# Moving spreading matmuls, column sums, roots and staged tiles in the plan of a hybrid encoder kernel

## The chip, the cores and the metric

One core of a Trainium2 chip runs the whole kernel. The metric is the device time of one execution in microseconds (us). Engines: TensorE (PE) multiplies, VectorE (DVE), ScalarE (ACT) and GpSimd (POOL) do the elementwise work, SyncE (SP) issues most transfers, in its own order.

## The reference

2048 tokens of 1024 channels go through two layers. Each normalises, mixes tokens (layer 0 by windowed attention, layer 1 by latent attention), multiplies the mixer's output o by a gate silu(z), projects it (w_out), adds the residual, and then adds an embedding p, projected and gated by a second product (ple_w_gate) of the newly normalised stream. The stages of this change are, in each layer, from o and z to the next layer's input:

```python
    return (o * jax.nn.silu(z)) @ w_out
...
        h = h + y
        gate = jax.nn.sigmoid(rms_norm(h, ple_norm_g[i]) @ ple_w_gate[i])
        h = h + (p[i] @ ple_w[i]) * gate
    return rms_norm(h, final_norm_g)
```

and the first product of layer 1 (`proj = u @ w_in` in `mla`), in the stage called Latents below.

## The kernel before, in words

Everything is float32. A product of precise operands is three matmuls: each operand is split in a high and a low part, and `mm3` (L285, its matmuls L290 to L292) adds high by high, high by low and low by high. The stream is held transposed, channels on partitions, in tiles of 128 channels x 512 tokens; a *group* is 512 tokens, so there are four groups (tg) of eight tiles (f).

The program is a run of stages: projections and windowed attention, `Post` for layer 0, `Latents`, gates, the dense attention (`Dense`), `Post` for layer 1. `Post` has two halves. In the **front**, 32 products (4 groups x 8 tiles f) of 24 matmuls project the gated o; to each product VectorE adds the residual tile (`x_load` L804, `add`), ScalarE squares it, GpSimd adds up the squares of a group (`gather` L833), and the result is stored (L818). For groups 1 to 3 the attention's denominators must be spread over the 64 rows of each head: one *spreading matmul* per o tile (`o_spread`, L771) makes them from a row that `spread_load` (L753) brings and `spread_cut` (L763) splits; then `o_gate` (L778, L779) multiplies and `o_cut` splits o (L216 on ScalarE, L218). In the **back**, 32 products multiply the stored stream (`h_load` L887, `h_cut` L228 and L229) by the gate's weights; `mixin` scales (L922), takes the sigmoid (L927), multiplies by the embedding tile (`p_load` L904, multiply L929 on GpSimd), adds (L931) and squares (L827), `gather` L833 adds up again, `h_store` (L936) stores. In layer 1 the last group is cut in two segments of 256 columns.

For each group's norm, `sums_at` strings eight steps: the split of the added squares (`sum_split`, L216 and L218, tile blkE), two matmuls with ones (`sum_mm`, L266), a copy, a store of the row of 512 sums to memory, its read as 128 x 4 (`root_in` L862), the root in three steps (L236, ScalarE, L244 to L249), and the store of the roots (`root_out` L876, a 128 x 4 tile to 512 places of memory). The roots come back as a row on all partitions (`row_in`, L283). For the final layer `finish` (L940) multiplies by it; the very last segment does this without memory (`turn`, L950 to L987).

The order comes from `Plan`: each step is added with a time, `Plan.run` sorts by it and the steps are written out so; TensorE, VectorE, ScalarE and GpSimd keep that order. Times are in units of which 5.19 (`UNIT`) are one product. The order of SyncE's transfers is set by the scheduler, from when it takes each to be ready; SyncE then works in that order and waits where one isn't. Places in on-chip memory come from rings (`fring`), so a load into a place waits for the last reader of what lay there.

`Latents` begins where layer 0's back ends: 128 x 672 weight rows come through a ring of two places of 4 KB per partition (`stage`), which the first two token tiles (`u_load` L1130, `u_split`) and more weights (`cut_load`) share; each load is planned 4 units ahead of its split.

## Time and profile before

| | us |
|---|---|
| median of the 3 runs | 3672.93 (3672.21 to 3678.47) |
| the profiled execution: its own time | 3679.53 |
| its span in the trace | 3677.8 |
| TensorE busy | 3551.2 |
| VectorE, ScalarE, GpSimd busy | 2404.9, 2277.0, 1973.3 |

The table's busy times are of the whole span; the dense attention, from about 1700 to 3250 us of it, keeps its order but for one step. Layer 0's `Post` runs from about 840 to 1242 us of the span, the first products of `Latents` from there to 1265, layer 1's `Post` from about 3254 to the end. In a row of a timeline the bracket says how long the engine was idle before and what released it; SPq is SyncE's queue. In a row of windows the columns are the window's length, the busy time of each engine with its instructions, the granted clock of TensorE as a share of 2.4 GHz (PEclk), the mean share of the transfer engines that is busy, and GB/s.

### The profile page before, as it was taken

To read this page: it belongs to the slowest core of one execution; us is meant where nothing else is said; L and a number is where in the kernel's file an instruction comes from. 1 tells how busy PE (TensorE), PEld (TensorE's weight loads), DVE (VectorE), ACT (ScalarE), POOL (GpSimd) and SP (SyncE) were. 2 spreads that over 40 slices of the span, in tenths; PEclk is the share of its full clock that TensorE was granted. 3 is DMA by queue.
4 is the path that set the end of the run, shared out by engine and by line. 5 is a ranking of instruction groups with operands and counts; after the bars stand their busy time and mean duration, and the time that the engine had idled before them with its cause. 6 is when DMAs were issued, how large, how long until landed. Compare 5 with 4: busy or idle time off the path is not lost. (4 is left out here: it accounts for less than half of the span.)

```text
span 3677.8 us, 52432 instructions
## 1 busy us (share of the span) xinstructions
PE 3551.2 (97%) x17118; PEld 2967.2 (81%) x17118; DVE 2404.9 (65%) x4539; ACT 2277.0 (62%) x4267; POOL 1973.3 (54%) x1564
## 2 busy tenths in 40 slices
PE   8999999999899899999999999999999999989997
PEld 6888888877787798899888888888888888867776
DVE  6111169995444444514989898989898989964445
ACT  6111279994233433422989898989898989952333
POOL 5331310033333432111989898989898989953243
PEclk9999999999999999999999999999999999999998
DMA  5332378876654676654111212121212121066533
GB/s 189 134 118 89 106 208 203 199 193 200 165 142 133 162 220 220 224 163 131 36 51 35 54 36 59 35 58 36 57 36 58 36 63 36 26 193 178 173 97 106
DMA packets 380080, 428.18 MB, mean 116 GB/s; under 512 B 46287, under 2 KB 233167, under 8 KB 379102
## 3 DMA queue, kind: packets, MB, share of 16 engines
q1 hardware_dynamic: 360798, 390.75, 38.8%
q10 hardware_dynamic: 19008, 34.09, 2.5%
q8 instruction: 134, 2.20, 0.3%
q14 instruction: 140, 1.15, 0.1%
HBM read 251.65 MB, written 156.17 MB: 111 GB/s over the span
## 5 line engine op out<-in xcount | busy, mean ns | idle before, releaser
L1648 POOL TENSOR_TENSOR blkR<-blkF,blkX 128x512 fp32r<-128x512 f32 x1024 | 1351.6, 1333 | 177.8 <-PE ps L1638 51.7
L1609 DVE TENSOR_REDUCE blkF<-ps 128x1 f32<-128x512 f32 x1024 | 700.5, 684 | 77.4 <-PE ps L1605 41.6
L1640 ACT ACTIVATE blkF<-ps 128x512 f32<-128x512 f32 x1024 | 611.4, 597 | 100.1 <-PE ps L1638 51.1
L1641 ACT CAST blkX<-blkF 128x512 fp32r<-128x512 f32 x1024 | 635.5, 621 | 32.8
L1658 DVE TENSOR_TENSOR ps<-ps,blkF 128x512 f32<-128x512 f32 x896 | 615.5, 687 | 0.7
L1669 PE MATMUL ps<-blkR 128*128 128x512 f32 x1024 | 405.4, 396 | 1.1 <-POOL blkR L1648 1.1
L1668 PE MATMUL ps<-blkX,blkR 128*128 128x512 f32 x1024 | 405.2, 396 | 0.0
L290 PE MATMUL ps<-blkR 128*128 128x512 f32 (+2 forms) x888 | 341.2, 384 | 5.6 <-ACT blkR L216 5.4
L291 PE MATMUL ps<-blkR 128*128 128x512 f32 (+2 forms) x888 | 339.2, 382 | 0.6 <-DVE blkR L218 0.6
L292 PE MATMUL ps<-blkR 128*128 128x512 f32 (+2 forms) x888 | 338.9, 382 | 0.3 <-DVE blkR L218 0.3
L833 POOL TENSOR_TENSOR blkF<-blkF 128x512 f32<-128x512 f32 (+1 forms) x112 | 145.8, 1302 | 247.0 <-ACT blkF L827 236.8
L363 DVE TENSOR_TENSOR blkF<-ps,blkF 128x512 f32<-128x512 f32 x72 | 49.5, 691 | 301.4 <-PE ps L292 296.4
L218 POOL TENSOR_TENSOR blkR<-blkF,blkR 128x1024 fp32r<-128x1024 f32 (+1 forms) x39 | 73.5, 1889 | 305.6 <-ACT blkR L216 278.2
L1669 PEld LDWEIGHTS ps<-blkR 128*128 128x128 f32 x1024 | 194.7, 190 | 47.0 <-POOL blkR L1648 2.4
L1668 PEld LDWEIGHTS ps<-blkX,blkR 128*128 128x128 f32 x1024 | 194.9, 190 | 44.2
L827 ACT ACTIVATE blkF<-blkF 128x512 f32<-128x512 f32 (+1 forms) x120 | 72.2, 602 | 221.9 <-DVE blkF L812 112.3
L290 PEld LDWEIGHTS ps<-blkR 128*128 128x128 f32 x888 | 171.0, 193 | 36.9 <-ACT blkR L216 6.2
L292 PEld LDWEIGHTS ps<-blkR 128*128 128x128 f32 x888 | 170.5, 192 | 31.6 <-DVE blkR L218 1.0
L291 PEld LDWEIGHTS ps<-blkR 128*128 128x128 f32 x888 | 170.8, 192 | 29.7 <-DVE blkR L218 0.9
L223 DVE TENSOR_TENSOR blkR<-ps,blkR 128x512 fp32r<-128x512 f32 (+2 forms) x232 | 143.5, 625 | 48.9 <-ACT blkR L222 48.7
L1636 PE MATMUL ps<-blkZ 96*128 96x512 f32 x384 | 155.0, 404 | 7.8 <-ACT blkF L1640 7.8
L290 PE MATMUL ps<-blkR,blkX 128*128 128x512 f32 (+1 forms) x384 | 149.6, 390 | 11.9 <-ACT blkX L216 9.2
(272 smaller groups left out, 9030.2 us busy)
## 6 DMA issues: line engine op xcount, KB each, us to landing
h<-blkF SPq DMA_DIRECT2D x96, 256.0 KB
blkF<-h SPq DMA_DIRECT2D x80, 256.0 KB
a_qs<-blkF ACTq DMA_DIRECT2D x64, 256.0 KB
ple<-blkF SPq DMA_DIRECT2D x64, 256.0 KB
blkF<-h SPq DMA_DIRECT2D x32, 512.0 KB
b_v<-blkX SPq DMA_DIRECT2D x32, 512.0 KB
b_q<-blkX SPq DMA_DIRECT2D x64, 256.0 KB
blkZ<-b_q SPq DMA_DIRECT2D x64, 256.0 KB
```

Of the source, the lines that this page charges most:

```text
L290: mm(out, lhsT=lh, rhs=rh, start=(first and i == 0), stop=False)
L291: mm(out, lhsT=lh, rhs=rl, start=False, stop=False)
L292: mm(out, lhsT=ll, rhs=rh, start=False, stop=(last and i == n - 1))
L833: getattr(self.k.nc, eng).tensor_tensor(out=acc, in0=acc, in1=sq, op=ALU.add)
L1609: nc.vector.tensor_reduce(out=mm[:, qt, kc : kc + 1], in_=ps, axis=AX.X, op=ALU.max)
L1636: nc.tensor.matmul(sp, lhsT=kl[:, kt_], rhs=qh[0:96, :], start=True, stop=False)
L1640: nc.scalar.activation(pe, sp, AF.Exp, scale=SCALE_B)
L1641: nc.scalar.copy(ph, pe)
L1648: nc.gpsimd.tensor_tensor(out=pl, in0=pe, in1=fv(ph), op=ALU.subtract)
L1658: nc.vector.tensor_tensor(out=st["acc"], in0=prev, in1=st[kt][0], op=ALU.add)
L1668: nc.tensor.matmul(st["o"], lhsT=v, rhs=ph, start=(kt == 0), stop=False)
L1669: nc.tensor.matmul(st["o"], lhsT=v, rhs=pl, start=False, stop=(kt == NT - 1))
```

## The change

- `o_spread` of group 1 is put in pairs before products 3 to 6 of group 0; of a later group each before the product of the same number in the group before. Its loads, the spread row's load and split, and `o_cut` move with it.
- Roots and their stores are put 6 units later behind each column sum (`SUMS`); the front's column sums of groups 0 to 2 come 3 units later (`PS_SS`), the back's 3.5 (`PS_SB`), the back's gathers 2.15 (`GATHB`), `finish` 6 more, `x_load` 2.23 earlier, `h_load` of groups 1 to 3 two earlier.
- The ring of residual tiles (`xrs`) gets a fourth place, that of the second root row.
- `Latents`: weights in three places of 2.625 KB, the first token tile in two halves and the second in one piece with places of their own, and a table of load and split times (`L_AT0`).
- In `Dense` the last unit's reciprocal is put 4 units later.

```diff
@@ -33,19 +33,23 @@
...
 UNIT = 5.19
-PS_X, PS_EV, PS_ST, PS_SS, PS_H, PS_P, PS_HS, PS_SB = 2.17, 0.61, 2.06, 6.29, 1.2, 3, 0.68, 6.5
-L_FIRST, L_PACE, L_CUT = -32, 2.6, (9.44, 10.74, 22.24, 26.4, 32.24)
+PS_X, PS_EV, PS_ST, PS_SS, PS_H, PS_P, PS_HS, PS_SB = 4.4, 0.61, 2.06, 9.3, 1.2, 3, 0.68, 10
+L_AT = {c: 2.625 * (c % 3) for c in range(8)} | {("u", 0): (28, 36), ("u", 1): 0} | {("cut", "r", c): 5.25 for c in range(3)}
+L_AT |= {("cut", "v", 0): 0, ("cut", "v", 1): 4, ("cut", "q", 0): 0, ("cut", "q", 1): 4, ("cut", "q", 2): 0}
+L_AT0 = [(-36.2 + 2.65 * c, -30 + 2.65 * c) for c in range(8)] + [(-30, -9.5), (-11, 2.5)]
+L_AT0 += [(-10, -5), (-4.5, 0.5), (0.7, 6), (3, 9.44), (6.2, 10.74), (16, 22.24), (19, 26.4), (26, 32.24)]
+L_U2 = -14
 L_US, PS_SL = -0.33, 6.5
...
 PREP, PLE_LD = 3, 12
-PS_O1 = 15.5
 PS_WL, PS_OL, PS_OL2, PS_HL, PS_R1, PS_R2 = 4, 4, 3.72, 3.96, 2.57, 3
-L_LD, L_UL, L_KR, L_VS, L_QS, L_NS = 4, 4, 3, 1.8, 1.8, 1.8
+L_UL, L_KR, L_VS, L_QS, L_NS = 4, 3, 1.8, 1.8, 1.8
 G_WL, G_UL, G_R, G_ST = 4.5, 4.5, 3.5, 2.2
...
 D_LAT, D_RR, D_W = 19, 20, 21
-SUMS = (3, 4.2, 5, 7.5, 10.5, 10.7, 13, 14)
+SUMS = (3, 4.2, 5, 7.5, 16.5, 16.7, 19, 20)
+CUTAT, GATHB = (2.7, 1.9), 7.05
 G_W, G_U = (-15.79, -9, 2, 8), -9.81
...
@@ -693,7 +697,7 @@
...
         self.selspot = ("R", 92) if self.final else ("Y", 12)
-        self.xrs, self.sqs, self.faccs, self.baccs = k.fring(18, 20, 22), k.fring(26), k.fring(24, 14), k.fring(*baccs)
+        self.xrs, self.sqs, self.faccs, self.baccs = k.fring(18, 20, 22, rows[1]), k.fring(26), k.fring(24, 14), k.fring(*baccs)
         self.lasts = k.fring(4, 6)
...
@@ -864,16 +868,16 @@
...
-            self.st["r"] = self.k.root_end(self.st["root"], out)
+            self.st["r", i, g] = self.k.root_end(self.st["root", i, g], out)
...
@@ -1021,22 +1025,23 @@
...
                 if tg > 0:
-                    to = NC8 * (tg - 1) * UNIT + (PS_O1 + 3.2 * f if tg == 1 else 4.7 * f + 4)
-                    add(to - PS_OL2 - (4.2 if tg > 1 else 3.3), self.o_load, tg, f)
-                    add(to - 0.6, self.o_spread, tg, f)
+                    before = 3 + f // 2 if tg == 1 else NC8 * (tg - 1) + f
+                    to = (3 + f / 2 if tg == 1 else before) * UNIT + 0.6
+                    add(to - PS_OL2 - (6 if tg > 1 else 1.3), self.o_load, tg, f)
+                    add(before * UNIT - 0.01, self.o_spread, tg, f)
                     add(to, self.o_gate, tg, f, "both")
-                    add(to + 1.9, self.o_cut, tg, f, "both")
+                    add(to + CUTAT[tg > 1], self.o_cut, tg, f, "both")
                     if f == 0:
-                        add(to - 7, self.spread_load, tg)
-                        add(to - 2, self.spread_cut, tg)
-            self.sums_at(add, NC8 * (tg + 1) * UNIT + PS_SS, 1, tg)
+                        add(to - 9, self.spread_load, tg)
+                        add(to - 4.5, self.spread_cut, tg)
+            self.sums_at(add, NC8 * (tg + 1) * UNIT + (PS_SS if tg < NG - 1 else 6.29), 1, tg)
         t = NG * NC8 * UNIT
...
                 th = tb - NC8 * UNIT + (0.5 + 0.8 * f if tg == 0 else 1.2 + 0.75 * f) * UNIT + PS_H
-                add(th - PS_HL, self.h_load, tg, f)
+                add(th - PS_HL - (0 if tg == 0 else 2), self.h_load, tg, f)
                 add(th, self.h_cut, tg, f)
...
@@ -1047,7 +1052,11 @@
...
                     add(te + dt, self.mixin, g, f, i)
-                add(te + (4.9 if n == TG else 3), self.gather, 2, g, f, "vector" if last else "gpsimd")
+                if last or g == len(self.segs) - 1 and f == NC8 - 1:
+                    dt = 4.9 if n == TG else 3
+                else:
+                    dt = GATHB if n == TG else 3.7
+                add(te + dt, self.gather, 2, g, f, "vector" if last else "gpsimd")
                 t += unit
...
@@ -1068,7 +1077,7 @@
...
             if self.final and n == TG:
-                fin = t + PS_SB + 20
+                fin = t + PS_SB + 26
                 add(fin - 3, self.row_in, 2, g)
...
@@ -1098,7 +1107,7 @@
...
         self.k = k
-        self.stage, self.xts, self.cfs = k.fring(0, 4), k.fring(8, 21), k.fring(29, 32)
+        self.xts, self.cfs = k.fring(8, 21), k.fring(29, 32)
         self.uhs, self.uls = k.ring(("R", 36), ("R", 44)), k.ring(("R", 40), ("R", 48))
...
@@ -1111,8 +1120,7 @@
...
     def load(self, key, src):
-        wf = self.stage.tile([P, D])
-        wf = wf[:, : src.shape[-1]]
+        wf = self.k.at(("F", L_AT[key]), [P, src.shape[-1]])
         self.k.nc.sync.dma_start(wf, src)
...
@@ -1126,13 +1134,22 @@
...
         k = self.k
-        xt = (self.stage if t < 2 else self.xts).tile([P, NC8, P])
-        k.nc.sync.dma_start(xt, k.h1[:, t * P : (t + 1) * P].rearrange("(c p) t -> p c t", p=P))
-        self.st["u", t] = xt
+        src = k.h1[:, t * P : (t + 1) * P].rearrange("(c p) t -> p c t", p=P)
+        if t == 0:
+            xs = [k.at(("F", kb), [P, 4, P]) for kb in L_AT["u", 0]]
+        else:
+            xs = [k.at(("F", L_AT["u", 1]), [P, NC8, P]) if t == 1 else self.xts.tile([P, NC8, P])]
+        n = NC8 // len(xs)
+        for i, x in enumerate(xs):
+            k.nc.sync.dma_start(x, src[:, n * i : n * i + n])
+        self.st["u", t] = xs
     def u_split(self, t):
-        self.us[t] = self.uhs.tile([P, NC8, P], F32R), self.uls.tile([P, NC8, P], F32R)
-        self.k.split_sbuf(self.st.pop(("u", t)), *self.us[t])
+        u = self.us[t] = self.uhs.tile([P, NC8, P], F32R), self.uls.tile([P, NC8, P], F32R)
+        xs = self.st.pop(("u", t))
+        n = NC8 // len(xs)
+        for i, x in enumerate(xs):
+            self.k.split_sbuf(x, *[v[:, n * i : n * i + n] for v in u])
...
@@ -1321,12 +1338,10 @@
...
-        first = [(self.w_load, self.w_split, c) for c in range(NC8)] + [(self.u_load, self.u_split, 0)]
         cuts = [(self.cut_load, self.cut, w, c) for w, n in (("r", 3), ("v", 2), ("q", 3)) for c in range(n)]
-        first += cuts[:3] + [(self.u_load, self.u_split, 1)]
-        times = [L_FIRST + L_PACE * i for i in range(len(first))] + list(L_CUT)
-        for t, (load, cut, *args) in zip(times, first + cuts[3:]):
-            add(t - L_LD, load, *args)
+        first = [(self.w_load, self.w_split, c) for c in range(NC8)] + [(self.u_load, self.u_split, i) for i in range(2)] + cuts
+        for (t0, t), (load, cut, *args) in zip(L_AT0, first):
+            add(t0, load, *args)
             add(t, cut, *args)
...
@@ -1338,7 +1353,7 @@
...
                 if t + 2 < NT:
-                    add(e - L_UL, self.u_load, t + 2)
+                    add(L_U2 if t == 0 else e - L_UL, self.u_load, t + 2)
                     add(e + (L_US if t == 0 else 0.5), self.u_split, t + 2)
...
@@ -1751,8 +1766,9 @@
...
             plan.add(t0 + NT + DENAT + DLAG, self.spread, u)
-            plan.add(t0 + NT + RECIPAT, self.recip, u)
-            plan.add(t0 + NT + RECIPAT + ILAG, self.store_recip, u)
+            tr = t0 + NT + RECIPAT + (4 if u == nu - 1 else 0)
+            plan.add(tr, self.recip, u)
+            plan.add(tr + ILAG, self.store_recip, u)
             if h % 2 == 1 and h + 1 < HEADS and g < 2:
```

Three places show how the rows move. (In the changed kernel's file the same lines have numbers higher by 4, from L1130 on by more: L876 is L880, L1116 is L1124, L1130 is L1144.)

SyncE in the middle of layer 0's front, around the store of group 0's roots (`rs`) and the read of its row; L737 and L734 load z and o tiles for the spread groups, L804 residuals, L818 stores, L717 a weight. Before:

```order
L737 DMA blkF<-a_z 128x512
L876 DMA rs_94<-blkF 128x4x1
L734 DMA blkF<-a_o 128x512
L818 DMA h_85<-blkF 128x512
L283 DMA blkF<-rs_94 128x512
L804 DMA blkF<-in_c_xT 128x512
L737 DMA blkF<-a_z 128x512
```

and after:

```order
L741 DMA blkF<-a_z 128x512
L822 DMA h_85<-blkF 128x512
L880 DMA rs_94<-blkF 128x4x1
L738 DMA blkF<-a_o 128x512
L808 DMA blkF<-in_c_xT 128x512
L287 DMA blkF<-rs_94 128x512
L741 DMA blkF<-a_z 128x512
L822 DMA h_85<-blkF 128x512
L738 DMA blkF<-a_o 128x512
```

Before, the z and o tile right ahead of and behind the store are number 6 of group 2; after, all of group 2's tiles are ahead and the o tile between store and read is group 3's first.

GpSimd at the start of layer 0's back: L779 is the last gate of the front, L833 (L837) the gathers, L929 (L933) the multiplies by the embedding. Before:

```order
L779 TENSOR_TENSOR blkF<-blkF 128x512
L833 TENSOR_TENSOR blkF<-blkF 128x512 x9
L929 TENSOR_TENSOR blkF<-blkF 128x512 x2
L833 TENSOR_TENSOR blkF<-blkF 128x512
L929 TENSOR_TENSOR blkF<-blkF 128x512
```

and after:

```order
L783 TENSOR_TENSOR blkF<-blkF 128x512
L837 TENSOR_TENSOR blkF<-blkF 128x512 x9
L933 TENSOR_TENSOR blkF<-blkF 128x512 x3
L837 TENSOR_TENSOR blkF<-blkF 128x512
L933 TENSOR_TENSOR blkF<-blkF 128x512
```

A product's gather stood right behind its own multiply's chain and ahead of the next multiply; now it stands behind the next product's.

SyncE at the end of layer 0's back; L1116 (L1124) are the weights of Latents, L1130 (L1144) its token tiles, L904 (L908) embedding tiles, L936 (L940) stores, L876 (L880) a store of roots. Before:

```order
L1116 DMA blkF<-in_b_w_in 128x672
L1130 DMA blkF<-h_87 128x8x128
L904 DMA blkF<-ple_83 128x512
L1116 DMA blkF<-in_b_w_in 128x672
L936 DMA h_87<-blkF 128x512
L876 DMA rs_95<-rcol 128x4x1
L1116 DMA blkF<-in_b_w_in 128x672
L1145 DMA blkF<-in_c_rope 128x512
L904 DMA blkF<-ple_83 128x512
L1116 DMA blkF<-in_b_w_in 128x672
L936 DMA h_87<-blkF 128x512
L1130 DMA blkF<-h_87 128x8x128
```

and after, the first token tile's two halves:

```order
L1124 DMA blkF<-in_b_w_in 128x672
L1144 DMA blkF<-h_87 128x4x128
L908 DMA blkF<-ple_83 128x512
L940 DMA h_87<-blkF 128x512
L1124 DMA blkF<-in_b_w_in 128x672
L908 DMA blkF<-ple_83 128x512
L940 DMA h_87<-blkF 128x512
L1144 DMA blkF<-h_87 128x4x128
L1124 DMA blkF<-in_b_w_in 128x672
```

and further on the second token tile:

```order
L1162 DMA blkF<-in_c_rope 128x512
L880 DMA rs_95<-rcol 128x4x1
L908 DMA blkF<-ple_83 128x512
L940 DMA h_87<-blkF 128x512
L1144 DMA blkF<-h_87 128x8x128
```

The first token tile's load stood behind five weights, and now its halves stand behind the second and third; the second's stood 6 rows behind the store of roots and now stands 3 behind it, with the third tile's load ahead of both (not shown).

## Rows read from the trace of the kernel before

**Rows 1.** The page, busy time of each engine (its share of the span)

```profile
PE 3551.2 (97%) x17118; PEld 2967.2 (81%) x17118; DVE 2404.9 (65%) x4539; ACT 2277.0 (62%) x4267; POOL 1973.3 (54%) x1564
```

**Rows 2.** TensorE's timeline, three places: start, length, line, operation, [idle before <-releaser]

```profile
876.13 0.39 PE L290 MATMUL ps<-blkR 128*128 128x512 f32 x1
...
881.80 0.39 PE L290 MATMUL ps<-blkR 128*128 128x512 f32 x1
...
897.59 0.65 PE L771 MATMUL ps<-blkY 128*128 128x512 f32 x1 [2.56 <-DVE blkY L763]
898.03 0.63 PE L290 MATMUL ps<-blkZ,blkR 128*128 128x512 f32 x1
...
3663.91 0.28 PE L291 MATMUL ps<-blkR,blkY 128*128 128x256 f32 x1
3664.03 0.28 PE L292 MATMUL ps<-blkR,blkY 128*128 128x256 f32 x1
```

**Rows 3.** Windows of the six stages, as the table's text explains

```profile
887.46:1047.19 159.73, 144.43 (x600) 116.24 (x598) 73.01 (x98) 46.04 (x72) 52.33 (x39) 0.95 0.71 173
1091.22:1241.76 150.54, 140.60 (x584) 113.95 (x583) 62.85 (x96) 58.89 (x89) 58.06 (x45) 0.94 0.54 146
1241.76:1265.30 23.54, 15.12 (x76) 13.90 (x75) 10.35 (x12) 11.19 (x20) 16.24 (x13) 0.85 0.60 184
3304.69:3454.12 149.43, 140.47 (x599) 114.01 (x598) 73.53 (x98) 46.03 (x72) 52.25 (x39) 0.98 0.66 177
3498.15:3598.45 100.30, 92.75 (x389) 74.72 (x388) 48.08 (x72) 35.85 (x56) 37.76 (x30) 0.97 0.34 97
3598.45:3677.80 79.35, 55.54 (x395) 53.31 (x393) 42.49 (x101) 26.92 (x55) 27.04 (x31) 0.84 0.36 110
```

**Rows 4.** Waits of TensorE, layer 0's front: us in total, times, longest

```profile
PE ps L771 <- DVE blkY L763: 5.0, 2, 2.6
...
PE ps L266 <- DVE blkE L218: 3.2, 1, 3.2
```

**Rows 5.** SyncE's timeline in layer 0's front

```profile
924.38 0.38 SPq L876 DMA_DIRECT2D rs<-blkF  x1
...
934.70 0.32 SPq L283 DMA_DIRECT2D blkF<-rs  x1
```

**Rows 6.** GpSimd's timeline at the same place

```profile
936.49 1.28 POOL L779 TENSOR_TENSOR blkF<-blkF 128x512 f32<-128x512 f32 x1 [4.63 <-DMA blkF<-a_o]
```

**Rows 7.** Waits of TensorE, layer 0's back

```profile
PE ps L266 <- ACT blkE L216: 9.7, 3, 4.5
```

**Rows 8.** Timeline of all engines at the first column sum of layer 0's back

```profile
1099.81 0.68 DVE L922 TENSOR_TENSOR blkF<-ps,blkF 128x512 f32<-128x512 f32 x1
...
1103.86 0.69 DVE L922 TENSOR_TENSOR blkF<-ps,blkF 128x512 f32<-128x512 f32 x1
...
1104.75 1.26 POOL L833 TENSOR_TENSOR blkF<-blkF 128x512 f32<-128x512 f32 x1 [1.53 <-ACT blkF L827]
...
1106.04 0.62 ACT L216 CAST blkE<-blkF 128x512 fp32r<-128x512 f32 x1 [1.44 <-POOL blkF L833]
```

**Rows 9.** Waits of TensorE, the start of Latents

```profile
PE ps L290 <- ACT blkR L216: 4.0, 1, 4.0
```

**Rows 10.** ScalarE's timeline there, the split of the second token tile

```profile
1254.03 1.04 ACT L216 CAST blkR<-blkF 128x1024 fp32r<-128x1024 f32 x1 [1.78 <-DMA blkF<-h]
```

**Rows 11.** Waits of TensorE, the last 16 products and the end

```profile
PE ps L970 <- DVE blkF L249: 9.5, 2, 7.4
```

**Rows 12.** The chain that ended last: start, length, step

```profile
3629.08 9.97 DMA rs<-blkF
...
3639.07 5.42 DMA blkF<-rs
...
3667.07 0.44 DVE blkF L833
```

**Rows 13.** VectorE's timeline at the same place

```profile
3644.51 0.75 DVE L940 SCALAR_TENSOR_TENSOR blkZ<-blkZ,gam,blkF 128x512 f32<-128x512 f32 x1 [0.26 <-DMA blkF<-rs]
```

14 lines of the change are left out of this document (7 added, 7 removed).

## The prediction

> **What bounds the kernel now.** I read the head of the page first: TensorE is busy for 97% of the span [rows 1] of 3677.8 us, which is 1.7 us less than the profiled execution's own time of 3679.53 us. So TensorE is the bound, and what a change of order can give is the time in which TensorE stands still or runs slowly. Next I took its full pace from its timeline: a product of 24 matmuls of 512 columns and the one spreading matmul behind it take 5.67 us (881.80 - 876.13) [rows 2]. That is 0.2267 us an instruction, 5.44 us a product. Behind a wait of 2.56 us the pace is half: 0.44 us from 897.59 to 898.03 [rows 2]. The windows show such slow stretches as granted clocks of 0.84 to 0.98 in the mean [rows 3], a mix of the two levels of 2.4 and 1.2 GHz.
>
> The stages that the change touches have a window each. Instructions times 0.2267 us, taken from the window's length, is what was lost there: layer 0's front groups 1 to 3, 159.73 - 600 x 0.2267 = 23.7 us; its back groups 1 to 3, 150.54 - 584 x 0.2267 = 18.1; layer 1's front, 149.43 - 599 x 0.2267 = 13.6; its back groups 1 and 2, 100.30 - 389 x 0.2267 = 12.1. The first three products of Latents are 72 matmuls of 336 columns (0.149 us each by that pace) and 4 others: 23.54 - 11.6 = 11.9. The last 16 products are half as wide, 0.12 us a matmul (3664.03 - 3663.91) [rows 2]: they take 3664.15 - 3598.45 = 65.7 us where 384 x 0.12 and 1.1 for seven others would do, 18.5 lost; behind the last of them come 13.65 us to the end of the span. Sum: **98 us** that can be had. It is more than the waits alone, since the slow pace behind them counts too.
>
> What ends the waits? In layer 0's front it is mainly these. L771, the spreading matmul, waits twice, 5.0 us in all, for the last operation of its row's split (L763), and L266, the column sum, 3.2 us for its accumulator's [rows 4]. Other products (L290) wait for o tiles that were cut late, and behind that stands SyncE's queue: the root's write L876 is issued at 924.38, the row's read L283 can't go until 934.70 because it reads what was written, and SyncE takes its work in order, so every load behind stands still for 10 us [rows 5]. The o tile whose load was issued between the two keeps GpSimd waiting 4.63 us, to 936.49 [rows 6]. So a write of 2 KB, in 512 elements of four bytes, costs some 10 us of queue and slows the transfers beside it.
>
> The Trainium skill, DMA: Bandwidth & Descriptors, section Anatomy of one DMA, fits one transfer by about 2.0 us and its bytes over 436 GB/s; by it this write would be over in 2 us, and moving it would bring nothing. The rows measured 10.3 us from issue to the read behind it, so here the trace decides.
>
> **The change, part by part.**
>
> *Front products (both layers).* The same matmuls are issued; none is added or taken away. Group 1's spreading matmuls now stand in pairs before products 3 to 6 of group 0, the others singly before the product of the same number, and their row's load and split 2 to 2.5 units earlier (a unit of the plan is about 1.05 us, since 5.19 units are one product of 5.44). The row's split came 2.5 us late twice [rows 4]; 2.5 units take all of that. Roots go 6 units later, so the root's write stands behind the loads of group 2's last tiles, not ahead of them. The order shows it: after, one o, one x load stand between write and read, and all of group 2's z and o tiles are ahead. The 10 us of queue stay, but the loads behind are then those of group 3's tiles, used a group (43.5 us) on. The column sum goes one product later: 5.44 us against 3.2 us waited; TensorE's next product covers it. x loads go 2.23 units earlier with a fourth place in their ring; that place is the second row's, so this row's read moves behind the last x store, at the start of back group 0 and a group (43.5 us) ahead of its first use. I cost it at nothing: back group 0 hides it, and without that cover it is the 5.42 us of a row's read [rows 12]. Bounds: 0 (every wait moves on) to 23.7 + 13.6. Each wait that I named gets more room than it lasted, which lies near the upper end; an eighth I leave for slow starts: **21 + 12**.
>
> *Back products.* Column sums wait 9.7 us in 3, the longest 4.5 [rows 7]. Why: group 0's last product ends at 1091.22 [rows 3], its gather L833 starts at 1104.75, 13.5 us later, where the plan has 5.5 units; the accumulator's split begins when it ends, 1106.04. VectorE is catching up, since its evacuations L922 start 4.05 us apart and products end 5.44 apart [rows 8]. The change does two opposite things: the sum goes 3.5 units later, which the order turns into one whole product, 5.44 us; but the gather goes 2.15 units later too, behind the next product's multiply L929. While the engines lag, that multiply's operand is there, and it costs its 1.3 us: net 5.44 - 1.3 = 4.1 us, against waits of 3.2 in the mean and 4.5 at most. Without the lag it would come a product later and net 1.4 units, but then the sum waits for nothing. A square's place in its ring of three is asked back 3.35 units after the gather, so nothing waits for that. Bounds 0 to 18.1; near the upper one, less the slow starts that are left, I take three quarters, **14**. In layer 1, where the h loads come 2 units earlier, late h splits are part of the 12.1; **8** of it.
>
> *Latents.* ScalarE's split of the second token tile waits 1.78 us for its load, and TensorE 4.0 us for the split [rows 9, 10]. After, the first two tiles have places of their own and are loaded 20.5 and 13.5 units ahead of their splits, not 4; the order shows the first one's halves ahead of most weights. The second's load still stands behind a root's write, and its split is 3.3 units later. Weights use three places of 2.6 KB, not two of 4, so a load waits for the split three before it, not two. Bounds 0 to 11.9; I take 70%, **8**.
>
> *End of layer 1.* The chain goes through the root's write (9.97 us) and the read of the row (5.42 us) [rows 12]; from 3644.51 VectorE has eight finishing steps L940 of 0.75 us [rows 13] in the midst of the next group's root, and L970 waits for that, 7.4 us at the longest [rows 11]. After, the row is read behind the ple load before the last four, and lands by my estimate some 48.5 us after the start of the last 16 products (now 46.1: 3644.51 - 3598.45), near the last product. VectorE's steps from there (8 x 0.75 = 6 us, and as much of the last products' own) take 12 us, and from the last gather to the end it is 10.7 us as now (3677.80 - 3667.07) [rows 12]. 48.5 + 12 + 10.7 = 71.2 us against 79.35 [rows 3]: **8**, a half of the 18.5 that TensorE alone could save, since here VectorE, not TensorE, would end last. Bounds: all of 18.5, or 6 lost if the steps stand wholly behind the present end.
>
> *Dense.* The last unit's reciprocal goes 4 units later. Group 3 of layer 1 needs it first, 16 products (87 us) on, and these hide it: 0.
>
> Sum: 21 + 12 + 14 + 8 + 8 + 8 = 71. From this I take 11 for waits that the order lets me expect in place of the old: rows (2,0) and (2,1) still come to VectorE with 8 steps (6 us) ahead of a column sum (2 each), the second token tile (2), and the slow pace after such half-cured stalls (5, 0.21 us an instruction more for 24). **Forecast: 60 us less.** The profiled execution is 6.6 us over the median of the runs shown, 3672.93; against the median, 3613.
>
> **The rivals.**
> - *The front alone (18%).* Back sums and the end don't gain: the lag moves with the sum, since the gather was moved with it. For: both were moved, by 2.15 and 3.5 units. Against: in TensorE's order the sum moved by a whole product. Then 21 + 12 + 8 and less 3 for new waits = 38: 3673 - 38 = 3635.
> - *New waits take most (8%).* The earlier loads meet the weights' in the front (DMA share 0.71 there [rows 3]) and o tiles land late; the front gains half of its 33, the rest is lost to the same in the back: 15, 3658.
> - *Nothing moves (5%).* The root's block lies elsewhere in the queue and stalls something else there. Against: each wait gets more room than it lasted. Within 7.3 us of 3673. By the Trainium skill's fit (above) it would be so too, since a write of 2 us holds nothing up; the trace's 10.3 us speak against it.
> - *Slower (5%).* Eleven root writes have a row's read behind them (four front groups in either layer, three back groups of layer 1). If what is queued behind each is needed at once, 10.3 us each is 113 us, against the 98 now lost: 15 more, 3688. It decides from 98/11 = 8.9 us uncovered at each. For: the later place is nearer to the read in the back groups, where the next h and p loads are behind it. Against: those loads have 2 units more, and before, where the write was as long, all the stalls together came to 98.
>
> **The numbers.** The forecast's own case has 64%. Its range, by the bounds above, is a gain of 45 to 83: 3590 to 3628. With the front alone, and half of the smaller gains, the range goes to 3648 (a gain of 25). A measurement of this kernel tells 0.2%, 7.3 us, from no change. Faster: 64 + 18 + 8 = 90%; same 5%; slower 5%.
>
> **What would show it.** Right: the same windows come out at 139 and 138 us (front), 137 (layer 0's back), 15 (Latents), the granted clock of the fronts goes to 0.98 or more, the rows L771 and L266 leave the list of waits or fall under 1 us; SyncE's row read still stands 10 us behind its write, with nobody waiting; the end's L970 waits under 2 us. Wrong: L266 keeps 2 to 4 us a time in the back groups (the lag moved along), L290 waits for o or h splits behind SyncE's block, or the last product is followed by over 16 us of finishing. If the fronts gain under 20 together, my reading of the root's write as their cause is wrong.

## The result and the profile after

The changed kernel takes 3625.4 us (median of 4 runs, 3623.12 to 3625.78) where the kernel before takes 3675.7 on the same chip (4 runs, the profiled one among them): 0.9861 of it, 95% interval 0.9849 to 0.9873, or 50 us less. Measured once more on another chip it was 0.9878 (0.9862 to 0.9895), 44 us less. Forecast were 60 us less, with a range from 25 to 83.

The same six windows as in [rows 3], of the changed kernel, in the same order; the columns are the same.

```profile
884.95:1020.47 135.52, 135.52 (x598) 112.08 (x597) 70.13 (x94) 43.71 (x68) 49.71 (x37) 1.00 0.69 201
1064.50:1198.93 134.43, 133.15 (x583) 109.09 (x582) 79.39 (x93) 57.81 (x89) 61.11 (x45) 1.00 0.60 162
1198.93:1221.69 22.76, 14.23 (x76) 13.44 (x74) 12.38 (x15) 11.04 (x20) 14.64 (x15) 0.78 0.59 167
3262.67:3398.15 135.48, 135.48 (x598) 112.09 (x597) 68.84 (x93) 43.33 (x67) 48.77 (x37) 1.00 0.65 189
3442.18:3538.73 96.55, 91.03 (x389) 74.50 (x388) 60.65 (x69) 36.06 (x56) 43.10 (x30) 0.96 0.31 91
3538.73:3623.70 84.97, 52.76 (x395) 50.17 (x393) 47.82 (x102) 25.16 (x52) 27.40 (x29) 0.81 0.36 112
```

Both fronts run from end to end at 100% of the clock with TensorE busy for the whole window: 24.2 and 13.95 us less. Layer 0's back gives 16.1. The start of Latents gives 0.8, layer 1's back 3.75, and the last stage is 5.6 us **longer**. Together that is 53.2 of the 54.1 us between the two spans (3677.8 and 3623.7); of the rest, 2.5 us were gained ahead of the first window and 1.6 lost between the two layers. So the gain came where it was forecast in both fronts and in layer 0's back; at Latents it did not come, and in layer 1's back and end together 1.9 us were lost.

What waits are left? TensorE's waits of the changed kernel, first from 1190 to 1240 us, the start of Latents, then from 3420 us to the end:

```profile
PE ps L294 <- ACT blkR L220: 6.7, 1, 6.7
```

```profile
PE ps L954 <- DVE blkF L837: 13.5, 1, 13.5
PE ps L270 <- ACT blkE L220: 11.7, 2, 6.2
```

L771 and L266 (now L775 and L270) are gone from the fronts' lists, as was to be seen. But L270 stands 11.7 us in the second back, where the kernel before's same wait (L266) came to 6.2, and the last column sum (L954) stands 13.5 us behind the last product. VectorE's timeline shows where it stands, at the first finishing step L944 of each row:

```profile
3490.10 0.75 DVE L944 SCALAR_TENSOR_TENSOR blkF<-blkF,gam 128x512 f32<-128x512 f32 x1 [3.77 <-DMA blkF<-rs]
...
3544.84 0.75 DVE L944 SCALAR_TENSOR_TENSOR blkZ<-blkZ,gam,blkF 128x512 f32<-128x512 f32 x1 [5.94 <-DMA blkF<-rs]
...
3599.50 0.75 DVE L944 SCALAR_TENSOR_TENSOR blkZ<-blkZ,gam,blkF 128x512 f32<-128x512 f32 x1 [7.03 <-DMA blkF<-rs]
```

Each time VectorE stands 3.8 to 7.0 us until the row has come from memory, with the evacuations of the back products behind it in its queue. In the kernel before it stood there too, longer for the first two rows and not for the third, which is the one that [rows 13] shows (0.26 us):

```profile
3540.06 0.75 DVE L940 SCALAR_TENSOR_TENSOR blkF<-blkF,gam 128x512 f32<-128x512 f32 x1 [9.64 <-DMA blkF<-rs]
...
3592.37 0.75 DVE L940 SCALAR_TENSOR_TENSOR blkZ<-blkZ,gam,blkF 128x512 f32<-128x512 f32 x1 [8.99 <-DMA blkF<-rs]
```

In all it is 18.9 us before and 16.7 after. What is new is the third wait, and that the finishing steps stand nearer to the next column sum: they were put 9.5 units later, the sum 3.5.

### The profile page after: what moved, and what is told of

Its sections match the earlier page's. It is cut to its first block, busy times and chain, and to the rows that moved or that the text cites. A ratio compares the mean times of both kernels' runs of the same rounds, so it can differ in the third digit from the quotient of the medians.

```text
span 3623.7 us, 52443 instructions
## 1 busy us (share of the span) xinstructions
PE 3522.8 (97%) x17118; PEld 2949.7 (81%) x17118; DVE 2453.7 (68%) x4539; ACT 2277.4 (63%) x4268; POOL 1987.7 (55%) x1565
## 4 chain that ended last, share of the span: by engine, by line
PE 84%; DVE 6%; DMA 3%; ACT 2%; issue 2%; POOL 1%; SPq 0%; ACTq 0%; DVEq 0%; POOLq 0%
PE ps L296 13%; PE ps L294 13%; PE ps L295 13%; PE ps L1620 7%; PE ps L1653 6%; PE ps L1651 6%; PE ps L1683 6%; PE ps L1652 6%; PE ps L1684 6%; PE ps L601 2%; PE ps L615 1%; DVE blkF L935 1%; PE ps L557 1%; PE ps L556 1%; PE ps L616 1%
## 5 line engine op out<-in xcount | busy, mean ns | idle before, releaser
L222 POOL TENSOR_TENSOR blkR<-blkF,blkR 128x512 fp32r<-128x512 f32 (+1 forms) x40 | 74.0, 1855 | 302.2 <-ACT blkR L220 274.9
L1684 PEld LDWEIGHTS ps<-blkR 128*128 128x128 f32 x1024 | 195.0, 190 | 46.9 <-POOL blkR L1663 2.3
L837 POOL TENSOR_TENSOR blkF<-blkF 128x512 f32<-128x512 f32 (+1 forms) x112 | 159.5, 1424 | 99.3 <-ACT blkF L831 98.3
L933 POOL TENSOR_TENSOR blkF<-blkF 128x512 f32<-128x512 f32 (+1 forms) x70 | 85.8, 1225 | 223.2 <-ACT blkF L931 192.5
L294 PEld LDWEIGHTS ps<-blkR 128*128 128x128 f32 x888 | 168.0, 189 | 34.5 <-ACT blkR L220 3.1
L296 PEld LDWEIGHTS ps<-blkR 128*128 128x128 f32 x888 | 167.6, 189 | 31.6 <-DVE blkR L222 1.2
L295 PEld LDWEIGHTS ps<-blkR 128*128 128x128 f32 x888 | 167.9, 189 | 28.2
```

The lines of the kernel that those rows point to most:

```text
L294: mm(out, lhsT=lh, rhs=rh, start=(first and i == 0), stop=False)
L295: mm(out, lhsT=lh, rhs=rl, start=False, stop=False)
L296: mm(out, lhsT=ll, rhs=rh, start=False, stop=(last and i == n - 1))
L1684: nc.tensor.matmul(st["o"], lhsT=v, rhs=pl, start=False, stop=(kt == NT - 1))
```

## The experiments

Twelve kernels ran; each ratio is to the kernel before, run beside it. Windows of a stage are compared with a second trace of the changed kernel, from the run `changed_again`, since they repeat to 2 us where whole runs on different chips differ by more.

**The changed kernel again.**

> The changed kernel itself once more, for a comparison on the same chip as the other runs of this call. All theories: a ratio to the kernel before of 0.986 within 0.003, and stage windows within 1.5 us of the first trace's (front groups 1 to 3 135.5 and 135.5, back of layer 0 134.4, start of Latents 22.8, last stage 85).

Measured: 3620.74 us, 0.9878 (0.9862 to 0.9895). Its windows of layer 0's back, the start of Latents, layer 1's back and the last stage:

```profile
1062.95:1195.61 132.66, 132.43 (x584) 109.18 (x582) 78.56 (x91) 56.69 (x87) 61.05 (x46) 1.00 0.58 158
1195.61:1217.68 22.07, 14.73 (x75) 13.95 (x74) 12.86 (x17) 11.56 (x21) 13.39 (x14) 0.77 0.57 176
...
3438.26:3533.11 94.85, 90.02 (x389) 73.78 (x388) 59.31 (x69) 36.09 (x56) 41.03 (x29) 0.98 0.32 92
3533.11:3618.60 85.49, 53.20 (x395) 50.81 (x393) 48.88 (x102) 25.17 (x52) 27.68 (x30) 0.83 0.36 111
```

The windows are the same within 1.8 us, a little over the 1.5 expected.

**The spreading matmuls put back.**

```diff
-before = 3 + f // 2 if tg == 1 else NC8 * (tg - 1) + f
-to = (3 + f / 2 if tg == 1 else before) * UNIT + 0.6
+to = NC8 * (tg - 1) * UNIT + (15.5 + 3.2 * f if tg == 1 else 4.7 * f + 4)
...
-add(before * UNIT - 0.01, self.o_spread, tg, f)
+add(to - 0.6, self.o_spread, tg, f)
...
-add(to - 4.5, self.spread_cut, tg)
+add(to - 2, self.spread_cut, tg)
```

> The changed kernel with the spreading matmuls, their loads, gates and cuts put back where they stood before; all else as changed. Theory S (the places of the spreading matmuls and the earlier split of their row cured the front): the waits of the spreading matmul for its row's split, some 5 us in two, come back in either layer, with their slow starts; the windows of front groups 1 to 3 go from 135.5 us each to 143 to 150, the time goes up by 12 to 25 us. Theory R (the root's write in SyncE's queue was the cause): the windows stay within 3 us of 135.5, the time within 6 us of the changed kernel's.

Measured: 3649.03 us, 0.9959 (0.9944 to 0.9974), 30 us of 44 given back. The fronts' windows, and TensorE's waits there in layer 0 and in layer 1 (before the change: [rows 3, 4]):

```profile
885.13:1032.29 147.16, 139.24 (x600) 113.04 (x598) 67.31 (x96) 44.67 (x70) 52.02 (x38) 0.99 0.68 186
...
3275.85:3417.79 141.94, 138.20 (x599) 113.08 (x598) 68.15 (x96) 44.91 (x70) 52.94 (x38) 0.99 0.65 185
```

```profile
PE ps L775 <- DVE blkY L767: 4.4, 2, 2.6
```

```profile
PE ps L775 <- DVE blkR L767: 2.6, 1, 2.6
```

Theory S holds in the main: the first wait, 2.6 us as before, is back in both layers, and the fronts cost 11.7 and 6.5 us more. In layer 1 it is one wait, not two, and the window stays a microsecond under the 143 expected. This is a half of what the fronts gained (24.2 and 13.95). The run puts the loads, gates and cuts of the o tiles back too, so the other half, which it leaves cured, does not hang on their places alone. The time rose by more than the 12 to 25 us expected: of the 25.5 us between this trace's span and the changed kernel's the fronts are 18 and the back products some 7.

**The fronts' roots put back.**

```diff
-for dt, (f, *args) in zip(SUMS, steps):
+for dt, (f, *args) in zip((3, 4.2, 5, 7.5, 10.5, 10.7, 13, 14) if i == 1 else SUMS, steps):
```

> The changed kernel with the fronts' roots, their stores and the reading of the row put back (6 units earlier); the back's stay. Theory R (the root's write, 10 us of SyncE's queue ahead of needed o tiles, was the cause of the second half of the front's stalls): the front window of layer 0 goes from 135.5 to 144 to 148, layer 1's to 139 to 142, the time up by 12 to 17 us. Theory S (the spreading matmuls' places are what counts; the earlier loads of o tiles cover a 10 us block anyway): both windows within 2 us of 135.5, the time within 4 us.

Measured: 3648.61 us, 0.9961 (0.9949 to 0.9973). The price came, but in another place. Layer 0's front and back, and layer 1's back:

```profile
886.29:1023.33 137.04, 136.13 (x599) 111.90 (x597) 61.28 (x83) 40.45 (x63) 44.34 (x35) 1.00 0.65 188
1074.08:1215.37 141.29, 135.91 (x584) 110.65 (x582) 82.38 (x96) 59.98 (x92) 64.67 (x48) 0.98 0.56 160
...
3458.94:3561.10 102.16, 92.12 (x390) 74.88 (x388) 64.34 (x74) 38.52 (x60) 45.66 (x32) 0.95 0.31 88
```

The fronts lose 1.5 us and nothing. What loses is the back: layer 0's groups 1 to 3 8.6 us and layer 1's 7.3, and the first groups, which lie ahead of those windows, 6.7 (50.75 in place of 44.03, by the products' starts) and 3.0 (47.04 in place of 44.02). That is 25 of the 28 us between this run and the changed kernel's. So Theory S holds for the fronts' windows, and its "time within 4 us" falls. Theory R is not decided by it, since the edit hardly moved the root's write: the first is issued 34.8 us after the window's start (921.04) where the changed kernel's stands 36.0 behind it (919.44 - 883.44), the second within 0.3 us of its place, and the third comes 10 us later. VectorE shows why. Its idle time before a root's first step (L240), until the sums have been read from memory, in all and in how many times, of the changed kernel and then of this one; and the third of these waits in layer 0:

```profile
  DMA blkF<-sq: 20.9, 6
```

```profile
  DMA blkF<-sq: 66.6, 8
```

```profile
1019.96 0.17 DVE L240 TENSOR_SCALAR blkF<-blkF 128x4 f32<-128x4 f32 x1 [11.85 <-DMA blkF<-sq]
```

The step asks for the sums before they have come, VectorE keeps its order, and the evacuations behind it wait: 11.85 us at one time, at the root of group 2. In the kernel before these waits came to 20.3 us in 9, though the roots stood as near to their sums as here. VectorE was late there: to the first of these steps it came 29.0 us after the window's start (916.41), and here after 21.6 us (917.12 less the 9.22 that it waited), with the sums there at 30.8. So over the whole trace the later roots did not shorten these waits; they kept them from growing now that VectorE is less late.

**One front root a layer put back, that of the last group.** The edit is the same with `i == 1 and g == NG - 1`.

> The changed kernel with one front root a layer put back 6 units earlier: that of the last group, whose read of the sums falls in the last front products. Theory V (what putting the fronts' roots back cost, 22 us in the back windows, comes from VectorE standing at that one root's first step until the sums' row is read from memory, 11.9 us there, just when the back's first splits are due): VectorE's wait there is 8 to 12 us again, layer 0's first back group 48 to 51 us in place of 44.0, its back groups 1 to 3 138 to 142 in place of 132.7, the time up by 12 to 22 us. Rival A (all four roots are needed for it): every window within 2 us of the changed kernel's.

Measured: 3628.35 us, 0.9885 (0.9868 to 0.9902), which alone is not distinguishable from the changed kernel. VectorE's wait at that step was 1.09 us in layer 0 and 2.99 in layer 1 (none in the changed kernel), not 8 to 12. Layer 0's first back group stayed at 44.02, groups 1 to 3 and layer 1's back cost 3.3 and 4.3 us:

```profile
1066.07:1202.03 135.96, 133.63 (x584) 109.00 (x583) 80.97 (x94) 57.91 (x89) 62.81 (x47) 1.00 0.59 160
...
3446.49:3545.64 99.15, 91.02 (x390) 73.99 (x389) 62.90 (x72) 37.27 (x58) 44.88 (x32) 0.97 0.32 91
```

```profile
1041.21 0.17 DVE L240 TENSOR_SCALAR blkF<-blkF 128x4 f32<-128x4 f32 x1 [1.09 <-DMA blkF<-sq]
```

My theory named the wrong root. The wait of 11.85 us (1019.96) falls ahead of the end of the front products (1023.33), so it is the root of group 2, which this run left in its later place. The last group's root makes 7.6 of the 25 us in the backs; the rest lies with the three roots ahead of it or with all four together, and no run put group 2's back alone.

**Layer 0's back roots put back.** The same with `i == 2 and not self.final`.

> The changed kernel with the back roots of layer 0 alone put back 6 units earlier. Theory V (the back's column sums were late because VectorE stood 2.0 to 2.7 us at each root's first step, waiting for the sums' read, as in the kernel before; with the roots later it doesn't): these waits come back, and with them waits of 1 to 4 us before a group's column sum, back groups 1 to 3 at 137 to 144 us in place of 132.7, the time up by 4 to 11 us. Rival B (in the back the roots' place is of no account; the gain came from the last front root and from the earlier loads of the stream): windows within 2 us, the time within 4 us.

Measured: 3635.17 us, 0.9909 (0.9892 to 0.9926), 0.3% over the changed kernel. The back of layer 0, and the longest of the three waits of VectorE at the root's first step that came back (the others are 1.41 and 1.57 us):

```profile
1065.64:1207.51 141.87, 135.53 (x584) 109.94 (x582) 74.77 (x91) 55.73 (x86) 56.39 (x43) 0.99 0.59 143
```

```profile
1192.02 0.17 DVE L240 TENSOR_SCALAR blkF<-blkF 128x4 f32<-128x4 f32 x1 [4.13 <-DMA blkF<-sq]
```

This window is 9.2 us longer, and the start of Latents 3.1 (25.19). The two intervals touch by a hair, so the windows decide, which repeat to 2 us. Theory V holds: in layer 0's back, where VectorE no longer waits for the sums at all, that is what the later roots are worth.

**The column sums put back, with the gathers.** Two runs: the gathers alone, and the sums with them, the roots' times kept.

```diff
-CUTAT, GATHB = (2.7, 1.9), 7.05
+CUTAT, GATHB = (2.7, 1.9), 4.9
...
-dt = GATHB if n == TG else 3.7
+dt = GATHB if n == TG else 3
```

> The changed kernel with the back's gathers put back 2.15 units earlier, ahead of the next product's multiply on GpSimd; the column sums stay a product later. Theory L (the sum's later place alone covers the lag; the gather's place costs or gives a microsecond): back windows within 2 us, the time within 4 us of the changed kernel's. Rival G (GpSimd, waiting for the square with the next multiply behind it, lengthens each product's chain, so the lag was cured by the gather's move): the back windows of layer 0 go from 134.4 to over 140, the time up by 8 to 15 us.

```diff
-PS_X, PS_EV, PS_ST, PS_SS, PS_H, PS_P, PS_HS, PS_SB = 4.4, 0.61, 2.06, 9.3, 1.2, 3, 0.68, 10
+PS_X, PS_EV, PS_ST, PS_SS, PS_H, PS_P, PS_HS, PS_SB = 4.4, 0.61, 2.06, 9.3, 1.2, 3, 0.68, 6.5
...
-for dt, (f, *args) in zip(SUMS, steps):
+for dt, (f, *args) in zip((3, 4.2, 5, 7.5, 20, 20.2, 22.5, 23.5) if i == 2 else SUMS, steps):
...
-fin = t + PS_SB + 26
+fin = t + PS_SB + 29.5
```

> The kernel with the gathers put back, and the back's column sums put back 3.5 units too; the steps of the roots behind them stay at the times they have in the changed kernel. So against the kernel with the gathers back alone only the sums and their way through memory move. Theory L (the back's gain came from TensorE reaching the sum a product later): the sums' waits come back, 2.5 to 4.5 us each in layer 0, that window goes from 132.1 to 142 to 150, layer 1's back groups 1 and 2 from 92.6 to 97 to 101, the time up by 12 to 22 us. Rival V (it came from VectorE, which no longer waits for the sums' read at the root's first step): both windows within 3 us, the time within 5 us.

Measured: 3612.27 us (0.9861, 0.9845 to 0.9878) and 3613.34 (0.9859, 0.9844 to 0.9873). The second ran beside the changed kernel and is 7.4 us faster; of the first, on another chip, the ratio says 6 us and the spans of the traces 7.5. The windows of layer 0's back, the start of Latents, layer 1's back and the last stage are 0.6, 2.2, 2.3 and 5.8 us less than the changed kernel's. Three of them, of the first:

```profile
1065.03:1197.11 132.08, 132.08 (x584) 109.27 (x582) 60.48 (x92) 56.74 (x87) 60.03 (x46) 1.00 0.60 160
...
3438.85:3531.41 92.56, 90.10 (x389) 73.89 (x388) 46.84 (x68) 36.12 (x56) 38.87 (x29) 0.98 0.33 94
3531.41:3611.10 79.69, 51.72 (x395) 49.38 (x393) 42.15 (x101) 24.65 (x51) 25.27 (x29) 0.85 0.37 119
```

and layer 0's back of the second:

```profile
1065.94:1198.69 132.75, 132.52 (x584) 109.20 (x582) 60.02 (x92) 57.39 (x89) 59.93 (x46) 1.00 0.59 160
```

Two expectations fell. That the sum comes a product later is worth nothing beside the later roots: with it put back the window is 132.75, within 0.7 us, so Theory L is refuted and V holds. And the gather's later place, thought to cost or give a microsecond, costs 6 to 7 us; by the windows more than half of it lies in the last stage. The mechanism stands in two rows. The changed kernel's GpSimd and VectorE at one product (timeline of all engines):

```profile
1067.30 1.29 POOL L837 TENSOR_TENSOR blkF<-blkF 128x512 f32<-128x512 f32 x1
1067.38 1.76 DVE L935 TENSOR_TENSOR blkF<-blkF 128x512 f32<-128x512 f32 x1 [2.07 <-POOL blkF L933]
```

GpSimd goes from the multiply straight into the gather, VectorE's add starts 0.08 us later and takes 1.76 us. With the gather put back the add stands alone and takes 0.69 us (1065.34). Over the 40 adds of this shape and place the groups of instructions say the same, of the changed kernel and of the one with the gathers back (busy time, mean ns):

```profile
L935 DVE TENSOR_TENSOR blkF<-blkF 128x512 f32<-128x512 f32 x40 | 58.8, 1469 | 42.9 <-POOL blkF L933 42.9
```

```profile
L935 DVE TENSOR_TENSOR blkF<-blkF 128x512 f32<-128x512 f32 x40 | 27.5, 688 | 53.2 <-POOL blkF L933 53.1
```

The gather's 1.29 and the add's own 0.69 one after the other make 1.98; less the 0.08 that had gone by, 1.90, so the 1.76 is nearly all of it: the two hardly overlap. The Trainium skill, SBUF — State Buffer, section SBUF: two separate sides, has it as a rule: VectorE and GpSimd share a port pair, held by one instruction to its end, and a VectorE operation with two inputs in SBUF needs it. The trace agrees here, with 0.69 us alone and 1.76 beside the gather. It does not agree wholly where the add begins 0.5 us behind the gather, as at 9 of the 24 gathers of the run `changed_again` from 1038 to 1189 us:

```profile
1071.87 1.74 POOL L837 TENSOR_TENSOR blkF<-blkF 128x512 f32<-128x512 f32 x1
```

```profile
1072.38 1.77 DVE L935 TENSOR_TENSOR blkF<-blkF 128x512 f32<-128x512 f32 x1
```

There GpSimd, which began first, takes 1.74 us in place of 1.29, and the two end 2.28 us after the start of the first, not 1.98.

**Layer 1's back roots put back, the finishing steps left late.** The edit of the roots with `i == 2 and self.final`.

> The changed kernel with the back roots of layer 1 alone put back 6 units earlier, while the finishing steps stay at their later place, so that a row has 12 units from its root's store to its first use, not 6. Theory W (VectorE waits for the row at the first finishing step, 3.8, 5.9 and 7.0 us, and what stands behind it makes the column sums and the end late): these waits shrink to under 3 us each, the column sums' waits of 5.5 and 6.2 us to under 3, the last stage from 85 us to 76 to 80, the time down by 10 to 16 us. Rival N (the eight finishing steps themselves, 6 us and more of VectorE, make it late, whenever the row comes): the sums wait as long, the time within 4 us of the changed kernel's.

Measured: 3616.65 us, 0.9871 (0.9857 to 0.9886), which alone is not distinguishable from the changed kernel. The expected 10 to 16 us did not come: the ratios say 3, the spans 2.7, and layer 1's back groups 1 and 2 stayed at 94.75. The trace is clear where the edit acts: VectorE's first finishing steps wait 1.01 and 1.55 us, the third not at all; the sums' waits shrink from 11.8 to 5.8 us; the last stage takes 78.33 us in place of 85.49. Against this 3.2 us more stand ahead of layer 0's windows and 1.4 between the layers, which the edit does not touch.

```profile
PE ps L270 <- ACT blkE L220: 5.8, 2, 3.5
```

```profile
3537.57:3615.90 78.33, 53.74 (x395) 51.22 (x393) 48.62 (x102) 25.27 (x52) 27.40 (x30) 0.84 0.37 120
```

Theory W holds for the waits and the last stage, with the sums' waits a little over what it said, perhaps since the gathers still lengthened VectorE's adds there; its time does not hold.

**Gathers, layer 1's column sums and roots put back together.** The edits of the gathers and of these roots, and:

```diff
-self.sums_at(add, t + (PS_SB if n * (g + 1) < T else PS_SL), 2, g)
+self.sums_at(add, t + ((6.5 if self.final else PS_SB) if n * (g + 1) < T else PS_SL), 2, g)
```

> The changed kernel with the gathers put back (worth 6 to 7 us alone) and, in layer 1's back, the column sums and roots put back to the times before, the finishing steps staying late, so that 15.5 units lie between a root's store and the row's first use. Theory W (a row that comes after VectorE asks for it is what stalls layer 1's back and end): no wait over 1 us for the first two rows, the column sums' waits under 2 us, back groups 1 and 2 at 88 to 92 us, the last stage 8 to 13 us shorter than the changed kernel's 85; the time 14 to 20 us under the changed kernel's of the last call, 3601 to 3607 if the kernel before runs at 3665. Rival N (VectorE's own work sets the pace): the time within 4 us of the kernel with the gathers put back, 3612.

Measured: 3601.92 us (3600.62 to 3604.95), 0.9818 (0.9803 to 0.9832). This is faster than both kernels: 66 us under the kernel before on that chip. Layer 1's back and the last stage, and TensorE's waits in them:

```profile
3438.01:3526.07 88.06, 88.06 (x390) 72.82 (x388) 50.13 (x71) 36.57 (x57) 38.81 (x29) 1.00 0.38 107
3526.07:3600.60 74.53, 52.56 (x395) 50.42 (x393) 42.74 (x99) 24.27 (x51) 25.43 (x29) 0.87 0.38 116
```

```profile
PE ps L974 <- DVE blkF L253: 7.8, 2, 5.7
PE ps L954 <- DVE blkF L837: 5.2, 1, 5.2
PE ps L270 <- ACT blkE L220: 1.0, 1, 1.0
```

Layer 1's back now runs without loss too (88.06 us busy of 88.06), and no finishing step is shown waiting for its row. The one wait of 5.7 us before L974 goes back to an embedding tile (`ple`): its load was issued at 3552.64, 1.2 us behind a root's write (3551.40), and GpSimd stood 7.5 us for it, to 3564.40.

**The last full group's eight finishing steps on ScalarE and GpSimd.** The edit comes on top of those of the run before.

```diff
+if g == 2:
+    self.gain(g, f)
+    self.k.nc.gpsimd.tensor_tensor(out=hf, in0=hf, in1=self.st["row", 2, g], op=ALU.mult)
+    return
```

> As the run before, and the eight finishing steps of the last full group are done by ScalarE (the gain) and GpSimd (times the row) in place of VectorE. Theory E (behind the last product VectorE's queue is the bound: the eight steps of 0.75 us stand between the last segment's own): from the last product's start to the end 4 to 7 us less than in the run before. Rival P (GpSimd takes over as the bound, 1.3 us a step between the multiplies that each product waits for): the end within 2 us of the run before, or later.

Measured: 3605.96 us, 0.9827 (0.9813 to 0.9842), not faster than the same kernel without this edit (3601.92); TensorE's last column sum waits longer:

```profile
PE ps L958 <- DVE blkF L837: 9.7, 1, 9.7
```

It is 9.7 us in place of 5.2, and the last stage takes 77.40 us in place of 74.53: Rival P holds, that the end comes no earlier.

**Latents: the second token tile's split earlier, and the old staging.** In the first, `(-11, 2.5)` becomes `(-11, -0.6)` in the table of times; in the second the class `Latents` is that of the kernel before.

> The changed kernel with the split of the second token tile put 3.1 units earlier, two places up in ScalarE's order (ahead of the last product's sigmoid, a weight's cast and a square); its load stays. Theory O (ScalarE comes to this split late, because each back product's chain over three engines takes 7 us where a product takes 5.4; the load had landed long before): TensorE's wait of 6.7 us for the split goes under 2, the first three products of Latents from 22.8 us to 15 to 18, the time down by 4 to 8 us. Rival D (the load behind the root's write is what is late, as the prediction had it): the split then waits for its load, and the window stays within 2 us of 22.8.

> The changed kernel with the staging and the times of Latents as before the change (a ring of two 4 KB places, each load 4 units ahead of its split). Theory O (at the start of Latents the change only put one wait in the place of another, since ScalarE's order is what is late): start of Latents within 3 us of 22.8 and back groups 1 to 3 within 3 us of 134.4, the time within 4 us. Rival D (the staging did pay, beside the back products): the back's window or the start of Latents grow by 8 us or more together.

Measured: 3623.42 us (0.9885, 0.987 to 0.9899) and 3630.25 (0.9903, 0.9888 to 0.9918), both beside the changed kernel's 3620.74. The start of Latents, of the first and the second:

```profile
1199.88:1219.75 19.87, 13.85 (x76) 12.94 (x74) 12.13 (x12) 10.59 (x19) 13.20 (x11) 0.91 0.59 185
```

```profile
1196.88:1227.78 30.90, 16.14 (x75) 14.73 (x74) 17.68 (x18) 11.38 (x20) 16.81 (x13) 0.78 0.62 150
```

and of the first TensorE's waits there and the moved split on ScalarE:

```profile
PE ps L296 <- POOL blkR L222: 3.0, 1, 3.0
PE ps L270 <- DVE blkF L240: 2.0, 1, 2.0
```

```profile
1205.60 1.05 ACT L220 CAST blkR<-blkF 128x1024 fp32r<-128x1024 f32 x1 [0.33 <-DMA blkF<-h]
```

The split moved up: TensorE's wait for ScalarE (5.5 us without the edit) is gone. At its later place, then, the split was late by ScalarE's order; at its new place it waits 0.33 us for the load, which lands 5.7 us after the window's start, so an earlier place still would have found no load. GpSimd's part of the split (3.0) and the first column sum (2.0) took the place of the wait, 2.2 us of the window is all, and the time didn't fall: neither theory holds as it stands, Theory O in its cause and not in its price. With the old staging the window is 30.90 us in place of 22.07 and the time 9.5 us longer: the staging is worth 9 us in the changed program, and this run's Theory O, that it only put one wait in another's place, is refuted.

## Why the prediction was right, and where it wasn't

**Fronts: right in size, half shown in cause.** Forecast 21 and 12, measured 24.2 and 13.95. The spreading matmuls' part is shown, with the loads, gates and cuts of the o tiles: 11.7 and 6.5 come back with them. The other half, which the prediction put down to the step "behind that stands SyncE's queue: the root's write", is open: the run that was to put the write back hardly moved it. Nor did the change move it as far as the plan says, 9 units with the sum's 3. The first write is issued 36.0 us after the window's start (920.98 - 884.95), before it was 36.9 (924.38 - 887.46), when TensorE has begun 160 instructions in place of 136: one product later. The write is as long as was read: SyncE issues it at 920.98 and the next load but one at 931.96, and no product waits behind it.

```profile
920.98 0.38 SPq L880 DMA_DIRECT2D rs<-blkF  x1
...
931.96 0.33 SPq L808 DMA_DIRECT2D blkF<-in_c_xT  x1
```

The Trainium skill's fit that the prediction quotes for such a write is given in the section named there for transfers that GpSimd issues, and this one is SyncE's; the 9.97 us of [rows 12] are what counts here. What cured the second half of the front's stalls, the earlier x loads, the later sum, or earlier o loads and later roots as substitutes for each other, is not separated: no run undid these alone. The prediction's own test for its reading of the write, fronts that gain under 20 together, could not tell: a half of the 38 that they gained came by the spreading matmuls.

**Layer 0's back: right in size by luck, wrong in cause.** Forecast 14, measured 16.1. The step "net 5.44 - 1.3 = 4.1 us, against waits of 3.2" was void: beside the later roots the sum's product is worth nothing, and the gather's move costs. The term that it missed is the root: VectorE stood 2.24, 2.74 and 1.28 us for the sums at the roots' first steps in this back of the kernel before, with the products' evacuations behind it. With the roots put back there 9.2 of the some 16 us are lost again. That the lag of each product's chain over three engines comes from these stops, so that the sum at its end is what TensorE sees, is how I read it; what gave the other 7 us was not separated. The row of the wait named the last link, and the prediction stopped there.

**Latents: the term was right, and was taken back.** Forecast 8; the staging is worth 9 in the changed program, but the window shrank by 0.8 us only. The rows of the second token tile's split on ScalarE show why:

```profile
1211.57 0.63 ACT L931 ACTIVATE blkF<-blkF 128x512 f32<-128x512 f32 x1 [2.08 <-DVE blkF L926]
1212.10 1.03 ACT L220 CAST blkR<-blkF 128x1024 fp32r<-128x1024 f32 x1
```

It waits for no load by then (issued at 1196.05, that had landed some 6 us before if it took 9.5 us, as in the run with the split put earlier); it stands behind the last product's sigmoid, which waits for VectorE. TensorE, freed of 16 us of stalls in the back, reaches Latents that much earlier, and the evacuations of the last group (L926, 7.5 us apart from 1188.23 to 1210.85) don't. In the four traces with the gathers put back the window is 19.5 to 21.5, in six with them late and nothing else of this stage edited 21.1 to 22.8. That a stage which no longer stalls hands its lag to the next was the omitted step.

**End of layer 1: wrong in sign.** Forecast 8 for the back and 8 for the end, less 4 for rows that still come late; measured 3.75 and -5.6. The step "lands by my estimate some 48.5 us after the start of the last 16 products" sized it wrong, at 2.4 us later than before: the row came at 3599.50 - 3538.73 = 60.8 us, 14.7 later. From the root's first step to the row it is as before (19.9 and 19.4 us), but that step came 14.2 us later, 40.9 us (3579.59) in place of 26.7 (3625.14) after the stage's start; 10 of that are the 9.5 units by which the plan put sum and root back. Sum, root and finish went later together, so the time between root and finish stayed 6 units where a root's write and a row's read take 15 us (9.97 + 5.42) [rows 12], and VectorE's wait for the third row went from 0.26 to 7.0 us. The waits were charged 2 us a row; they came to 3.8 to 7.0, and the two first ones, 9.64 and 8.99 us in the kernel before, were not in the prediction at all, which read the third row's. The step left out beside it is the gather: with the gathers alone put back the last stage takes 79.69 us, with these roots alone 78.33, with both and the sums 74.53, against 85.49 as changed and 79.35 before. So either of the two moves is worth the loss. Two of the prediction's signs of being wrong came: the column sums wait 5.5 and 6.2 us a time in layer 1's back, and some 25 us of finishing follow the last product. Here the rival "the front alone" described it better than the forecast: the lag moved along.

**The sum.** The terms made 71. Measured by windows, the fronts gave 5 more than theirs and layer 0's back 2 more; Latents gave 7 less, layer 1's back 4 less and the end 14 less: 71 + 7 - 25 = 53, the windows' sum. The 11 taken off for new waits were right in kind, and 18 were needed on balance. That the 60 came so near is in part luck: the 25 us that Latents and layer 1's second half fell short were met by the 7 us that the fronts and layer 0's back gave beyond their terms, and by those 11. The slower rival needed 8.9 us uncovered at each of eleven writes: VectorE's wait for a row came to 3.8, 5.9 and 7.0 us at three, and TensorE waited for no write in the fronts.

## What to carry to other kernels

Where an engine works in a fixed order, a step that reads something back from memory belongs behind the time at which it can have come, as counted from the trace (here 15 us from a root's store to its row); moving store and use later together bought nothing here. A wait before the last link of a chain says only who was late: follow it back to the first engine that stood idle, since here the sums' waits in layer 0's back hung on VectorE standing at another step, and giving the named link more time had no effect. A step's place in the plan is not its place in time: put 6 units earlier, a root's write was issued 1.2 us earlier, since VectorE stood for the sums ahead of it; so look at the trace whether an edit moved what it was to move. And before an operation is moved beside another on VectorE and GpSimd, measure what the two take alone and together.

## What the runs showed of the hardware

VectorE's add of two 128x512 tiles takes 0.69 us alone and 1.76 us when GpSimd's add of the same size has begun 0.08 us before it; GpSimd's own takes 1.29 then, and 1.26 elsewhere [rows 8], so VectorE alone pays. When the add begins 0.5 us behind GpSimd's, GpSimd's takes 1.74 and the add 1.77, so both pay. A store of 512 single elements of four bytes to memory, 2 KB, took 9.97 us [rows 12], and what was issued 1.2 us behind one (3552.64) was there for GpSimd only at 3564.40, 11.8 us after its issue; that the store holds it up is likely by this, but no run took the store away.
